# A two-block transformer kernel: the first norm's transposes moved ahead of the norm's factor, and SBUF tiles padded to 64 bytes

## The chip, the cores and the metric

The kernel runs on one NeuronCore of a Trainium2 chip. The metric is the device time of one execution in microseconds. Five engines work side by side, each through its own queue in order: TensorE (PE, with the loading of its stationary operand shown apart as PEld), VectorE (DVE), ScalarE (ACT), GpSimd (POOL) and SyncE (SP), which here only issues DMA transfers.

## What is computed

A sequence of 256 tokens of width 2048 goes through two blocks, one after the other. Only the first lines matter for the change:

```
def rmsnorm(x, w):
    xf = x.astype(jnp.float32)
    y = xf * lax.rsqrt(jnp.mean(xf * xf, axis=-1, keepdims=True) + RMS_EPS)
    return (y * w.astype(jnp.float32)).astype(x.dtype)
...
    h = x
    for l in range(DEPTH):
        u = rmsnorm(h, mix_norm_w[l])
        p = u @ w_in[l]
        o_dn = deltanet_group(p[..., :DN_COLS], ...)
        o_rw = rwkv7_group(p[..., DN_COLS:], ...)
        h = h + jnp.concatenate([o_dn, o_rw], axis=-1).astype(h.dtype) @ w_out[l]
        h = h + memory_cross_attention(...)
        h = h + squared_relu_mlp(rmsnorm(h, ffn_norm_w[l]), ffn_w1[l], ffn_w2[l])
    return rmsnorm(h, final_norm_w)
```

The second block has a gated mixer and attention of its own, and 32 experts of which a router picks two for each token.

## The kernel before

Everything is in float32. To keep its precision at TensorE's fast float32r rate, each large product is made of three: an operand is split into a high part (rounded to float32r) and the low rest, and high by high, high by low and low by high are summed in PSUM. `wsplit` (L283) does this for weights: one DMA of up to 1 MB into a tile `raw` (three buffers), then by halves an ACT cast into `wh` (L294) and a DVE subtraction into `wl` (L295). `gemm_To` (L300) takes the weights as the stationary operand and the activations `uh`, `ul` (tiles `b`) as the moving one, 256 columns at a time; `gemm_No` (L326) takes activations as the stationary and 512 columns of `wh` or `wl` as the moving operand.

The program starts in `setup` (L212): SP issues four transfers of x (rows 0 to 127 and 128 to 255, each in two halves of 1024 columns) into one `b` tile, then the constants `cst` (128x1088, the unit matrix in its first 128 columns), then the parameters `prm`. `mixers` (L870) loads a few rows, makes small parameters on DVE, and calls `norm_T` (L804), which works in a strict sequence: ACT squares x in eight pieces of 512 columns and sums each (L345); DVE adds the sums and finds the inverse root by three Newton steps on a 128x2 tile (L262 to L280); ACT and DVE multiply x by it (L811, L813); `to_T` (L366) then transposes the scaled x by 128x128 blocks on PE (L259), two blocks a chunk, and of each of the 16 chunks ACT writes the high part times the norm's weight (L372) and DVE the low part (L373).

With `uh` and `ul` the first product runs, `gemm_To` on `win_s` (272 columns of weights, L882), one matmul of 256 columns after the other through 16 chunks of depth; its 16-column group gives the gates. After it come eight units of the mixers (`rw_unit`, `dn_head`), fed by further products of `win`, then w_out, cross attention, the FFN, the second block, and at the end the experts, whose weights stream in by DMA. Beside the mixers DVE accumulates a matrix-vector product of `wmod` rows (L835), whose DMAs (L834) stand between those of `raw` in SP's queue.

The order of the instructions on each engine is fixed when the program is built: a scheduler places them by its own estimate of when their inputs are ready, and each engine then goes through its list strictly in order. A tile's address comes from its pool: tiles of a pool lie behind one another, each rounded up to 32 bytes a partition. Small tiles at the head of the pool `const` (`biases` is 16 bytes, `dnw` 4) put what follows at an odd multiple of 32 bytes: `row`, `raw`, `wh`, `wl`, and `h` in the later stages. The `b` tiles, `cst`, the FFN's `fh`, `fl` and `mraw`, the experts' `mw` and `oh` lie at a multiple of 64.

Of the kernel before, what the change touches and what calls it, by code (L numbers as in the profile page):

```python
# [88 lines left out]
CST = {}  # L89
# [96 lines left out]


class Prog:
# [23 lines left out]
    def setup(self):  # L212
        nc = self.nc
        self.bp = self.pool("b16", 3)
        self.xt = self.b16()
        for tb in range(2):
            for q in range(2):
                nc.sync.dma_start(self.xt[:, tb, q * 1024:q * 1024 + 1024], self.ins["x"][tb * 128:tb * 128 + 128, q * 1024:q * 1024 + 1024])
        self.cp = self.pool("const")
        self.rawp = self.pool("raw", 3)  # L220
        self.hlp = self.pool("hl", 3)
        ncst = CST["second"][0]
        nprm = sum(n for _, n in PRM.values())
        self.cst = self.cp.tile([128, ncst], F32, name="cst")
# [572 lines left out]
    def load_rows(self):  # L797
# [4 lines left out]
        nc.vector.tensor_scalar(self.dnw, self.p("dn_w"), 0.5, None, ALU.mult)  # L802

    def norm_T(self, src, w, uh, ul):  # L804
        nc = self.nc
        rs = self.rstd(src)
        for tb in range(2):
            for q in range(2):
                s = slice(q * 1024, q * 1024 + 1024)
                if q:  # L810
                    nc.scalar.activation(src[:, tb, s], src[:, tb, s], AF.Copy, scale=rs[:, tb:tb + 1])  # L811
                else:
                    nc.vector.tensor_scalar(src[:, tb, s], src[:, tb, s], rs[:, tb:tb + 1], None, ALU.mult)  # L813
        self.to_T([src[:, tb] for tb in range(2)], w, uh, ul)

# [43 lines left out]
    def phase1(self):  # L859
        with ExitStack() as ctx:  # L860
            self.psum(ctx, 0, {"acc": 3, "rwa": 1, "rwb": 2, "dn": 1, "dns": 1})
            self.smp = ctx.enter_context(self.tc.tile_pool(name="small1", bufs=3))
            self.rwp = ctx.enter_context(self.tc.tile_pool(name="rwp", bufs=1))
            self.dnp = ctx.enter_context(self.tc.tile_pool(name="dnp", bufs=2))
            self.scores = [self.rwp.tile([128, 2, 2, 512], F32, name=f"sc{i}") for i in range(2)]
            for a in self.scores:
                self.nc.gpsimd.memset(a, 0.0)
            return self.mixers()

    def mixers(self):  # L870
        nc = self.nc
        b16 = self.b16
        xt = self.xt
        self.load_rows()
        self.rw_params()
        self.mod_init()
        r16 = lambda a: a.rearrange("p b (k t) -> p (b k) t", t=256)
        uh, ul = r16(b16(F32R)), r16(b16(F32R))
        self.norm_T(xt, lambda c: self.p("mix_w", c), uh, ul)
        oT = r16(b16())  # L880
        acc, acg = self.mx("acc"), self.mx("dn")
# [27 lines left out]
    def b16(self, dt=F32):  # L909
        return self.bp.tile([128, 2, D], dt, tag="b16", name="b16")  # L910
# [67 lines left out]
    def xattn(self):  # L978
        nc = self.nc
        r16 = lambda a: a.rearrange("p b (k t) -> p (b k) t", t=256)  # L980
        with ExitStack() as ctx:
            P = ctx.enter_context(self.tc.tile_pool(name="xa", bufs=2))
            uh, ul = r16(self.b16(F32R)), r16(self.b16(F32R))
# [47 lines left out]
    def ffn(self, extra):  # L1031
        nc = self.nc
        r16 = lambda a: a.rearrange("p b (k t) -> p (b k) t", t=256)
        with ExitStack() as ctx:
            P = ctx.enter_context(self.tc.tile_pool(name="ffn", bufs=2))
            uh, ul = r16(self.b16(F32R)), r16(self.b16(F32R))
# [44 lines left out]
    def phase2(self, oT):  # L1081
# [9 lines left out]
        self.b2ctx = ExitStack()  # L1091
        self.b2p = self.b2ctx.enter_context(self.tc.tile_pool(name="b2rows", bufs=1))
        with ExitStack() as ctx:
            self.modp = ctx.enter_context(self.tc.tile_pool(name="modp", bufs=2))
            for q in range(4):
# [57 lines left out]
    def block2(self):  # L1153
# [3 lines left out]
        with ExitStack() as ctx:  # L1157
            P = ctx.enter_context(self.tc.tile_pool(name="b2", bufs=1))
            gmw = P.tile([128, 4, 128], F32, name="gmw")
# [597 lines left out]
    def moe(self):  # L1757
        nc = self.nc
        with ExitStack() as ctx:
            self.mxtag = "mx"  # L1760
            self.g2row = self.row_slot()
            self.row_bcast(self.modc[:, 5], self.g2row)
            K = ctx.enter_context(self.tc.tile_pool(name="kept", bufs=1))
            P = ctx.enter_context(self.tc.tile_pool(name="moe", bufs=1))
            self.load_ahead(13, P)
# [104 lines left out]
```

## Time and profile before

| | |
|---|---|
| Time, median of 3 runs | 2305.26 us (2300.73 to 2313.14) |
| The profiled execution's own time | 2314.7 us, 9.4 us over that median |
| Its span from first to last instruction | 2312.6 us |
| Busy share of the span | PE 95%, PEld 73%, DVE 64%, ACT 39%, POOL 3% |
[...]
| DMA | 575 MB, 249 GB/s over the span |

The span is cut into stages by what the engines work on: the start up to the first product (0 to 24.7 us), the first product (to 42.4 us), the mixers (to about 640 us), w_out, attention and FFN (to about 1610 us), the second block's mixer, and the experts from about 1820 us on, where the DMA engines are nearly always busy. In the timelines, an instruction's line is that of the helper that issues it; times are microseconds from the start of the span. A row of the chain of waits is one link of the work that ended last. A busy PE is not a PE at its peak, since matmuls overlap.

### The profile page before, as it was taken

To read this page: it belongs to the slowest core of one execution; us is meant where nothing else is said; L and a number is where in the kernel's file an instruction comes from. 1 tells how busy PE (TensorE), PEld (TensorE's weight loads), DVE (VectorE), ACT (ScalarE), POOL (GpSimd) and SP (SyncE) were. 2 spreads that over 40 slices of the span, in tenths; PEclk is the share of its full clock that TensorE was granted. 3 is DMA by queue.
4 is the path that set the end of the run, shared out by engine and by line. 5 is a ranking of instruction groups with operands and counts; after the bars stand their busy time and mean duration, and the time that the engine had idled before them with its cause. 6 is when DMAs were issued, how large, how long until landed. Compare 5 with 4: busy or idle time off the path is not lost.

```text
span 2312.6 us, 40957 instructions
## 1 busy us (share of the span) xinstructions
PE 2189.3 (95%) x16697; PEld 1696.1 (73%) x16697; DVE 1490.6 (64%) x2556; ACT 893.1 (39%) x1445; POOL 60.8 (3%) x166
## 2 busy tenths in 40 slices
PE   6999999999999889999999999999999989888787
PEld 6888888888787779998988989988897542233222
DVE  6778887766668788777687687756657532222223
ACT  5444443444544445434434344445555310011000
POOL 1000000010000000000000000000000000000000
PEclk9999999999899999999999999999999999999998
DMA  7425443232278776786686786754445798999997
GB/s 252 147 95 181 158 163 134 95 113 93 74 264 312 266 275 250 277 310 259 247 316 251 280 290 253 277 184 170 164 148 199 293 401 367 408 390 425 426 425 319
DMA packets 101622, 575.23 MB, mean 249 GB/s; under 512 B 11548, under 2 KB 12700, under 8 KB 45880
## 3 DMA queue, kind: packets, MB, share of 16 engines
q1 hardware_dynamic: 101432, 572.60, 65.6%
q8 instruction: 132, 2.16, 0.4%
q14 instruction: 58, 0.48, 0.1%
HBM read 570.45 MB, written 2.10 MB: 248 GB/s over the span
## 4 chain that ended last, share of the span: by engine, by line
PE 78%; DMA 11%; DVE 7%; ACT 2%; issue 2%; SPq 0%; DVEq 0%; ACTq 0%
PE acc L255 45%; PE mx L255 31%; DMA mw<-wgu 4%; PE mx L259 2%; DMA mw<-wd 2%; DMA b<-wgu 2%; DVE wl L295 1%; DMA mraw<-wmod 1%; DMA raw<-wd 1%; DVE macc L835 1%; DMA row<-wmod 0%; DMA raw<-win_s 0%; DMA raw<-wout 0%; DVE b L373 0%; ACT wh L294 0%
## 5 line engine op out<-in xcount | busy, mean ns | idle before, releaser
L294 ACT CAST wh<-raw 128x1024 fp32r<-128x1024 f32 (+1 forms) x496 | 516.3, 1043 | 722.2 <-PE acc L255 536.5
L295 DVE TENSOR_TENSOR wl<-raw,wh 128x1024 fp32r<-128x1024 f32 (+1 forms) x496 | 600.4, 1214 | 205.7 <-ACT wh L294 201.9
L255 PE MATMUL acc<-b,wh 128*128 128x256 f32 x2560 | 467.7, 283 | 1.0 <-ACT b L372 1.0
L255 PE MATMUL mx<-b,wh 128*128 128x256 f32 (+1 forms) x2016 | 414.1, 295 | 0.7 <-ACT wh L294 0.7
L255 PEld LDWEIGHTS acc<-b,wh 128*128 128x128 f32 x2560 | 398.1, 189 | 3.2 <-ACT b L372 1.7
L255 PE MATMUL acc<-b,wl 128*128 128x256 f32 x1280 | 363.8, 284 | 0.8 <-DVE wl L295 0.7
L255 PEld LDWEIGHTS mx<-b,wh 128*128 128x128 f32 (+1 forms) x2016 | 320.2, 190 | 11.5 <-issue 3.3
L255 PE MATMUL mx<-b,wl 128*128 128x256 f32 (+1 forms) x1008 | 297.4, 295 | 0.8 <-DVE wl L295 0.8
L255 PEld LDWEIGHTS acc<-b,wl 128*128 128x128 f32 x1280 | 241.3, 189 | 1.6 <-DVE wl L295 1.4
L835 DVE SCALAR_TENSOR_TENSOR macc<-mraw,silc,macc 128x1024 f32<-128x1024 f32 x160 | 205.0, 1282 | 54.2 <-DMA mraw<-wmod 53.4
L255 PE MATMUL acc<-wh,fh 128*128 128x512 f32 x512 | 204.3, 399 | 0.0
L255 PE MATMUL acc<-wh,fl 128*128 128x512 f32 x512 | 202.2, 395 | 0.0
L255 PE MATMUL acc<-wl,fh 128*128 128x512 f32 x512 | 201.0, 393 | 0.0
L255 PEld LDWEIGHTS mx<-b,wl 128*128 128x128 f32 (+1 forms) x1008 | 191.4, 190 | 5.0 <-DVE wl L295 1.1
L255 PE MATMUL mx<-mw,xs 128*32 128x512 f32 (+1 forms) x512 | 126.3, 656 | 21.2 <-DMA mw<-wgu 21.1
L255 PE MATMUL acc<-wh,b 128*128 128x512 f32 x384 | 124.3, 402 | 1.0 <-ACT row L976 1.0
L255 PEld LDWEIGHTS acc<-wh,fl 128*128 128x128 f32 x512 | 96.1, 188 | 24.4
L255 PEld LDWEIGHTS acc<-wl,fh 128*128 128x128 f32 x512 | 96.2, 188 | 23.2 <-DVE wl L295 0.2
L255 PEld LDWEIGHTS acc<-wh,fh 128*128 128x128 f32 x512 | 96.1, 188 | 22.0
L255 PE MATMUL mx<-raw,xs 128*32 128x512 f32 (+1 forms) x328 | 95.9, 625 | 10.0 <-DMA raw<-wgu 10.0
L1590 DVE SCALAR_TENSOR_TENSOR eth<-eth,mx 128x256 f32<-128x256 f32 x9 | 3.8, 421 | 145.3 <-ACT eth L1589 145.3
L255 PEld LDWEIGHTS mx<-mw,xs 128*32 128x32 f32 (+1 forms) x512 | 26.9, 120 | 84.6 <-issue 43.8
(490 smaller groups left out, 2823.1 us busy)
## 6 DMA issues: line engine op xcount, KB each, us to landing
raw<-w SPq DMA_DIRECT2D x128, 1024.0 KB, 5.6
mraw<-wmod SPq DMA_DIRECT2D x160, 512.0 KB, 5.0
raw<-win SPq DMA_DIRECT2D x76, 1024.0 KB, 4.9
mw<-wgu SPq DMA_DIRECT2D x62, 1024.0 KB, 14.3
raw<-wgu SPq DMA_DIRECT2D x40, 1024.0 KB, 14.5
mw<-wd SPq DMA_DIRECT2D x28, 1024.0 KB, 14.5
raw<-wout SPq DMA_DIRECT2D x24, 1024.0 KB, 5.9
b<-wgu SPq DMA_DIRECT2D x23, 1024.0 KB, 10.8
```

What stands on the lines that cost most here:

```text
L255: return self.nc.tensor.matmul(out, lhsT=lhsT, rhs=rhs, start=start, stop=stop, skip_group_check=True)
L259: return self.nc.tensor.transpose(out, in_, self.ident[:k, :k])
L294: nc.scalar.copy(h[:, :n], rs)
L295: nc.vector.tensor_tensor(l[:, :n], rs, h[:, :n], ALU.subtract)
L835: nc.vector.scalar_tensor_tensor(a, b, self.silc[:, k:k + 1], a, ALU.mult, ALU.add)
L1590: nc.vector.scalar_tensor_tensor(th[:n], th[:n], 1.0, ps[:n, 0:256], ALU.add, ALU.mult)
```

## The change

Three things change at the start. `setup` loads the unit matrix (the first 128 columns of `cst`) ahead of x, x by halves of its columns (first half of both row blocks, then the second), then `prm`, and the rest of `cst` behind it. `norm_T` comes ahead of `load_rows`, `rw_params` and `mod_init` in the program, and is written anew: three matmuls of zeros come first; the squares are divided between ACT (first row block) and DVE (second); the transposes take x as it is, before its factor is known, into seven PSUM banks and, once the first is free, an eighth; the factor is laid along the row by two matmuls (a row sum of the unit matrix scaled by it, so that each partition has all 256 factors) and copied to a 128x256 tile `row` by ACT; and each chunk then takes three instructions where it took two: DVE multiplies transposed x by weight and `row` into `f` (L863), ACT casts `f` into `uh` (L864), DVE subtracts into `ul` (L865).

Besides, every pool hands out SBUF tiles through a class `Lines`, which widens a tile whose size is an odd multiple of 32 bytes to the next multiple of 64, and gives a view of it. All SBUF tiles then start at a multiple of 64 bytes.

```diff
+class Lines:
+    def tile(self, shape, dt, **kw):
+        n = int(np.prod(shape[1:]))
+        size = mybir.dt.size(dt)
+        full = -(-n * size // 64) * 64 // size
+        if -(-n * size // 32) % 2 == 0:
+            return self.pool.tile(shape, dt, **kw)
+        t = self.pool.tile([shape[0], full], dt, **kw)[:, 0:n]
...
-        return self.ctx.enter_context(self.tc.tile_pool(name=name, bufs=bufs, **kw))
+        return Lines(self.ctx.enter_context(self.tc.tile_pool(name=name, bufs=bufs, **kw)))
...
-        for tb in range(2):
-            for q in range(2):
+        self.cst = self.cp.tile([128, ncst], F32, name="cst")
+        nc.sync.dma_start(self.cst[:, 0:128], self.ins["cst"][:, 0:128])
+        for q in range(2):
+            for tb in range(2):
                 nc.sync.dma_start(self.xt[:, tb, q * 1024:q * 1024 + 1024], self.ins["x"][tb * 128:tb * 128 + 128, q * 1024:q * 1024 + 1024])
...
-        nc.sync.dma_start(self.cst, self.ins["cst"][:, :ncst])
         nc.sync.dma_start(self.prm, self.ins["prm"])
+        nc.sync.dma_start(self.cst[:, 128:ncst], self.ins["cst"][:, 128:ncst])
...
     def norm_T(self, src, w, uh, ul):
         nc = self.nc
-        rs = self.rstd(src)
+        t1 = lambda: self.rwp.tile([128, 256], F32, tag="t1", name="t1", bufs=12)
+
+        z = self.hlp.tile([128, 1024], F32, tag="wl", name="zero")[:, 0:512]
+        nc.vector.memset(z, 0.0)
+        ps = self.mx("dns")
+        for _ in range(3):
+            self.mm(ps, z[:, 0:128], z)
+        ss = self.smp.tile([128, 2, 4], F32, tag="ss", name="ss")
+        for q in range(4):
+            for tb in range(2):
+                junk = self.hlp.tile([128, 1024], F32, tag="wh", name="junk")[:, 0:512]
+                s = src[:, tb, q * 512:q * 512 + 512]
+                if tb:
+                    nc.vector.scalar_tensor_tensor(junk, s, 1.0, s, ALU.mult, ALU.mult, accum_out=ss[:, tb, q:q + 1])
+                else:
+                    nc.scalar.activation(junk, s, AF.Square, accum_out=ss[:, tb, q:q + 1])
+        rs = self.rstd_from(ss)
...
+        ts = [transposed(j, tag) for j, tag in enumerate(("acc", "acc", "acc", "rwa", "rwb", "rwb", "dn"))]
+        ps = self.mx("dns")
         for tb in range(2):
-            for q in range(2):
-                s = slice(q * 1024, q * 1024 + 1024)
-                if q:
-                    nc.scalar.activation(src[:, tb, s], src[:, tb, s], AF.Copy, scale=rs[:, tb:tb + 1])
-                else:
-                    nc.vector.tensor_scalar(src[:, tb, s], src[:, tb, s], rs[:, tb:tb + 1], None, ALU.mult)
-        self.to_T([src[:, tb] for tb in range(2)], w, uh, ul)
+            self.mm(ps[:, tb * 128:tb * 128 + 128], rs[:, tb:tb + 1].to_broadcast([128, 128]), self.ident, start=(tb == 0))
+        row = t1()
+        nc.scalar.copy(row, ps[:, 0:256])
+        for j in range(8):
+            for c in range(2):
+                k = j * 2 + c
+                f = t1()
+                nc.vector.scalar_tensor_tensor(f, ts[j][:, c * 256:c * 256 + 256], w(k), row, ALU.mult, ALU.mult)
+                nc.scalar.copy(uh[:, k, :], f)
+                nc.vector.tensor_tensor(ul[:, k, :], f, uh[:, k, :], ALU.subtract)
+            if j == 0:
+                ts.append(transposed(7, "acc"))
```

The built programs show where this puts the instructions. On DVE, the list before goes from the root's last step to the scaling of x, the 16 low parts of the norm, and then the low parts of the first weights:

```order
L278 SCALAR_TENSOR_TENSOR rs_y<-rs_b,rs_y 128x2
L813 TENSOR_SCALAR b_58<-b_58,rs_y 128x1024 x2
L373 SCALAR_TENSOR_TENSOR b_111<-mx,prm,b_110 128x256 x16
L295 TENSOR_TENSOR wl<-raw,wh 128x544 x3
L835 SCALAR_TENSOR_TENSOR row<-row,silc 128x512 x2
L295 TENSOR_TENSOR wl<-raw,wh 128x544
```

In the changed list 32 instructions stand in their place, 16 of L863 and 16 of L865 in alternating groups of three or four, and this is the end of them (`t` is `f`, `b_98` is `ul`, `b_97` is `uh`):

```order
L863 SCALAR_TENSOR_TENSOR t_253<-mx,prm,t_186 128x256
L865 TENSOR_TENSOR b_98<-t_245,b_97 128x256
L865 TENSOR_TENSOR b_98<-t_249,b_97 128x256
L865 TENSOR_TENSOR b_98<-t_253,b_97 128x256
L315 TENSOR_TENSOR wl<-raw,wh 128x544 x3
L888 SCALAR_TENSOR_TENSOR row<-row,silc 128x512 x2
L315 TENSOR_TENSOR wl<-raw,wh 128x544
```

The low parts of the weights (L295 before, L315 now) still come behind all of the norm's work on this engine. On PE, the first product's list before starts right behind the 32 transposes, with four matmuls on the first weights' high part and then one on `wl`:

```order
L259 MATMUL mx<-cst,b_58 128x128 x32
L255 MATMUL mx<-b_110,wh 128x256
L255 MATMUL mx<-b_111,wh 128x256
L255 MATMUL mx<-b_110,wh 16x256
L255 MATMUL mx<-b_111,wh 16x256
L255 MATMUL mx<-b_110,wl 128x256
```

Now the zeros, 28 transposes, the factor's two matmuls and the last four transposes stand ahead of it, and the product itself begins with the same five:

```order
L275 MATMUL mx<-zero 128x512 x3
L279 MATMUL mx<-cst,b_58 128x128 x28
L275 MATMUL mx<-cst,rs_y 128x128 x2
L279 MATMUL mx<-cst,b_58 128x128 x4
L275 MATMUL mx<-b_97,wh 128x256
L275 MATMUL mx<-b_98,wh 128x256
L275 MATMUL mx<-b_97,wh 16x256
L275 MATMUL mx<-b_98,wh 16x256
L275 MATMUL mx<-b_97,wl 128x256
```

What moved is the transposes, from behind the factor to ahead of it; the fifth matmul of the product still needs the first `wl`. On SP, a part of its list before, from the fourth transfer of `win_s` on:

```order
L834 DMA row<-wmod 128x512 x2
L287 DMA raw<-win 128x2048
L834 DMA row<-wmod 128x512
L287 DMA raw<-win 128x2048
L834 DMA row<-wmod 128x512
L287 DMA raw<-win 128x2048
L834 DMA row<-wmod 128x512 x3
L287 DMA raw<-win 128x2048
```

and the same part now:

```order
L887 DMA row<-wmod 128x512 x2
L307 DMA raw<-win 128x2048
L887 DMA row<-wmod 128x512
L307 DMA raw<-win 128x2048
L887 DMA row<-wmod 128x512 x2
L307 DMA raw<-win 128x2048
L887 DMA row<-wmod 128x512 x2
L307 DMA raw<-win 128x2048
```

The transfers are the same; the rows of `wmod` stand elsewhere between those of `win`. In the mixers, too, the scheduler places a number of instructions differently against one another; from w_out on the lists agree but for line numbers.

## Rows read from the trace of the kernel before

**Rows 1.** The page of the whole span: engines' busy time, then the chain's shares.
```profile
PE 2189.3 (95%) x16697; PEld 1696.1 (73%) x16697; DVE 1490.6 (64%) x2556; ACT 893.1 (39%) x1445; POOL 60.8 (3%) x166
...
PE 78%; DMA 11%; DVE 7%; ACT 2%; issue 2%; SPq 0%; DVEq 0%; ACTq 0%
```
**Rows 2.** The chain that ended last, first 60 us: start, length, what.
```profile
4.78 9.37 DMA raw<-win_s
...
14.95 6.00 PE mx L259 x26
...
21.49 2.49 DVE b L373 x6
...
23.98 0.64 DVE wl L295
...
24.66 17.73 PE mx L255 x137
...
46.88 3.60 DMA row<-wmod
```
**Rows 3.** Timeline, 0 to 45 us: start, length, engine, line, out<-in, count.
```profile
2.71 0.56 SPq L226 DMA_DIRECT2D cst<-cst  x1
...
8.61 0.60 ACT L345 ACTIVATE mx<-b 128x512 f32<-128x512 f32 x1 [1.27 <-DMA b<-x]
...
9.89 0.60 ACT L345 ACTIVATE mx<-b 128x512 f32<-128x512 f32 x1
...
11.26 0.16 DVE L360 TENSOR_REDUCE s<-ss 128x2 f32<-128x8 f32 x1 [10.31 <-ACT mx L345]
...
16.24 2.65 ACT L372 ACTIVATE b<-mx,prm 128x256 fp32r<-128x256 f32 x7
...
23.89 1.99 DVE L295 TENSOR_TENSOR wl<-raw,wh 128x544 fp32r<-128x544 f32 x3
...
25.80 1.53 DVE L835 SCALAR_TENSOR_TENSOR row<-row,silc 128x512 f32<-128x512 f32 x2
```
**Rows 4.** The same chain of waits, at 43 us: two subtractions of 256 columns.
```profile
43.04 0.76 DVE t L461 x2
```
**Rows 5.** Groups by shape, whole span: count, busy us, mean ns, idle before.
```profile
L255 PE MATMUL mx<-b,wh 128*128 128x256 f32 x1984 | 409.0, 295 | 0.7 <-ACT wh L294 0.7
...
L255 PE MATMUL mx<-oh,b 128*128 128x256 f32 x256 | 36.2, 290 | 4.6 <-DVE xs L1521 3.1 <-DVE h L1630 1.5
...
L378 DVE TENSOR_TENSOR y<-ey,y 128x512 fp32r<-128x512 f32 x36 | 24.7, 687 | 2.9 <-ACT y L377 1.4
...
L1055 DVE TENSOR_TENSOR fl<-fy,fh 128x512 fp32r<-128x512 f32 x32 | 20.6, 686 | 0.0
...
L1119 ACT CAST b<-tab 128x256 fp32r<-128x256 f32 x16 | 6.0, 403 | 2.4 <-DVE tab L1118 2.3
```
**Rows 6.** The page's DMA issues: count, KB each, us to landing.
```profile
mw<-wgu SPq DMA_DIRECT2D x62, 1024.0 KB, 14.3
...
raw<-wgu SPq DMA_DIRECT2D x40, 1024.0 KB, 14.5
```
**Rows 7.** Busy us (count) of each engine by stretch; PEclk is the granted clock.
```profile
22.00:24.00 2.00, 1.17 (x6) 0.62 (x6) 2.00 (x6) 2.00 (x6) 0.00 (x0) 1.00 0.00 0
...
24.00:26.00 2.00, 1.33 (x6) 1.27 (x7) 2.00 (x4) 0.54 (x1) 0.00 (x0) 0.58 0.00 0
...
28.00:30.00 2.00, 2.00 (x19) 1.87 (x18) 1.39 (x2) 0.56 (x2) 0.00 (x0) 1.00 0.77 249
...
1200.00:1240.00 40.00, 40.00 (x335) 39.96 (x334) 24.77 (x24) 16.86 (x19) 0.16 (x1) 1.00 0.70 256
...
1520.00:1560.00 40.00, 40.00 (x173) 32.15 (x172) 21.84 (x22) 14.79 (x15) 0.00 (x0) 1.00 0.54 185
```
**Rows 8.** Groups by shape again: two of the products with 512 moving columns.
```profile
L255 PE MATMUL acc<-wh,fh 128*128 128x512 f32 x512 | 204.3, 399 | 0.0
...
L255 PE MATMUL acc<-wh,b 128*128 128x512 f32 x384 | 124.3, 402 | 1.0 <-ACT row L976 1.0
```

More of the change, by code (lines that the diff above doesn't have):

```diff
@@ L184, in pack, with __init__ @@
     return o
+class Lines:
+    def __init__(self, pool):
+        self.pool = pool
+    def tile(self, shape, dt, **kw):
[5 more added lines that the diff above has]
+        t = self.pool.tile([shape[0], full], dt, **kw)[:, 0:n]
+        if len(shape) == 2:
+            return t
+        names = "abcd"[:len(shape) - 1]
+        return t.rearrange(f"p ({' '.join(names)}) -> p {' '.join(names)}", **dict(zip(names, shape[1:])))
 class Prog:
@@ L215, in setup @@
         self.xt = self.b16()
-        for tb in range(2):
-            for q in range(2):
+        self.cp = self.pool("const")
+        ncst = CST["second"][0]
+        self.cst = self.cp.tile([128, ncst], F32, name="cst")
+        nc.sync.dma_start(self.cst[:, 0:128], self.ins["cst"][:, 0:128])
+        for q in range(2):
+            for tb in range(2):
                 nc.sync.dma_start(self.xt[:, tb, q * 1024:q * 1024 + 1024], self.ins["x"][tb * 128:tb * 128 + 128, q * 1024:q * 1024 + 1024])
-        self.cp = self.pool("const")
         self.rawp = self.pool("raw", 3)
         self.hlp = self.pool("hl", 3)
-        ncst = CST["second"][0]
         nprm = sum(n for _, n in PRM.values())
-        self.cst = self.cp.tile([128, ncst], F32, name="cst")
         self.prm = self.cp.tile([128, nprm], F32, name="prm")
-        nc.sync.dma_start(self.cst, self.ins["cst"][:, :ncst])
         nc.sync.dma_start(self.prm, self.ins["prm"])
+        nc.sync.dma_start(self.cst[:, 128:ncst], self.ins["cst"][:, 128:ncst])
         self.biases()
@@ new lines, in norm_T, with transposed @@
+        rs = self.rstd_from(ss)
+        def transposed(j, tag):
+            t = self.mx(tag)
+            for c in range(2):
+                k = j * 2 + c
+                for tb in range(2):
+                    self.tr(t[:, c * 256 + tb * 128:c * 256 + tb * 128 + 128], src[:, tb, k * 128:k * 128 + 128])
+            return t
+        ts = [transposed(j, tag) for j, tag in enumerate(("acc", "acc", "acc", "rwa", "rwb", "rwb", "dn"))]
+        ps = self.mx("dns")
+        for tb in range(2):
+            self.mm(ps[:, tb * 128:tb * 128 + 128], rs[:, tb:tb + 1].to_broadcast([128, 128]), self.ident, start=(tb == 0))
@@ new lines, in norm_T @@
+        row = t1()
+        nc.scalar.copy(row, ps[:, 0:256])
+        for j in range(8):
+            for c in range(2):
+                k = j * 2 + c
+                f = t1()
[4 more added lines that the diff above has]
+                ts.append(transposed(7, "acc"))
@@ L861, in phase1 @@
             self.psum(ctx, 0, {"acc": 3, "rwa": 1, "rwb": 2, "dn": 1, "dns": 1})
-            self.smp = ctx.enter_context(self.tc.tile_pool(name="small1", bufs=3))
-            self.rwp = ctx.enter_context(self.tc.tile_pool(name="rwp", bufs=1))
-            self.dnp = ctx.enter_context(self.tc.tile_pool(name="dnp", bufs=2))
+            self.smp = Lines(ctx.enter_context(self.tc.tile_pool(name="small1", bufs=3)))
+            self.rwp = Lines(ctx.enter_context(self.tc.tile_pool(name="rwp", bufs=1)))
+            self.dnp = Lines(ctx.enter_context(self.tc.tile_pool(name="dnp", bufs=2)))
             self.scores = [self.rwp.tile([128, 2, 2, 512], F32, name=f"sc{i}") for i in range(2)]
@@ L873, in mixers @@
         xt = self.xt
+        r16 = lambda a: a.rearrange("p b (k t) -> p (b k) t", t=256)
+        uh, ul = r16(b16(F32R)), r16(b16(F32R))
+        self.norm_T(xt, lambda c: self.p("mix_w", c), uh, ul)
         self.load_rows()
@@ L981, in xattn @@
         with ExitStack() as ctx:
-            P = ctx.enter_context(self.tc.tile_pool(name="xa", bufs=2))
+            P = Lines(ctx.enter_context(self.tc.tile_pool(name="xa", bufs=2)))
             uh, ul = r16(self.b16(F32R)), r16(self.b16(F32R))
@@ L1091, in phase2 @@
         self.b2ctx = ExitStack()
-        self.b2p = self.b2ctx.enter_context(self.tc.tile_pool(name="b2rows", bufs=1))
+        self.b2p = Lines(self.b2ctx.enter_context(self.tc.tile_pool(name="b2rows", bufs=1)))
         with ExitStack() as ctx:
-            self.modp = ctx.enter_context(self.tc.tile_pool(name="modp", bufs=2))
+            self.modp = Lines(ctx.enter_context(self.tc.tile_pool(name="modp", bufs=2)))
             for q in range(4):
@@ L1157, in block2 @@
         with ExitStack() as ctx:
-            P = ctx.enter_context(self.tc.tile_pool(name="b2", bufs=1))
+            P = Lines(ctx.enter_context(self.tc.tile_pool(name="b2", bufs=1)))
             gmw = P.tile([128, 4, 128], F32, name="gmw")
@@ L1762, in moe @@
             self.row_bcast(self.modc[:, 5], self.g2row)
-            K = ctx.enter_context(self.tc.tile_pool(name="kept", bufs=1))
-            P = ctx.enter_context(self.tc.tile_pool(name="moe", bufs=1))
+            K = Lines(ctx.enter_context(self.tc.tile_pool(name="kept", bufs=1)))
+            P = Lines(ctx.enter_context(self.tc.tile_pool(name="moe", bufs=1)))
             self.load_ahead(13, P)
```

5 lines of the change are left out of this document (1 added, 4 removed).

## The prediction

> **What bounds the kernel now.** I read the page first. PE is busy for 2189.3 of 2312.6 us, and the chain that ended last lies on PE for 78% and on DMA for 11% [rows 1]. So time won or lost before PE's first product reaches the end almost whole: the mixers are a chain on PE, and the experts' stage cannot start before them. Next I read that chain over the first 60 us [rows 2]: x lands, ACT squares it (the row that names win_s covers the squares and the root), DVE scales, PE transposes from 14.95 us, DVE writes low parts until 23.98, then the first `wl`, and from 24.66 PE multiplies for 17.73 us without a break, until 42.40. This is the stretch that the change rewrites. What ends last in it is not PE but DVE: the product cannot get past its fifth matmul until DVE has made the first `wl`, and in DVE's list that stands behind all of the norm's work.
>
> **The start, step by step.** All times are of the profiled execution.
>
> 1. x. The transfer of the unit matrix goes ahead of x on SP; a transfer of `cst` took SP 0.56 us to issue [rows 3]. ACT waited for the third piece of x until 8.61 and took the fourth at 9.89 without a wait [rows 3], so the fourth had landed by 9.89 and now lands by about 10.4. `prm` moves ahead of the rest of `cst` and is there earlier than now; the rest of `cst` is wanted only after the first product, over 30 us later, so its delay costs nothing.
>
> 2. Squares. ACT's row block is first and ends earlier. DVE squares the fourth piece in two instructions of 512 columns; the nearest row is two products of that form in 1.53 us [rows 3]. So the sums are complete at about 11.9, against 11.26 now: dividing the squares gains nothing, since the last piece of x sets the end.
>
> 3. The root. From the reduction at 11.26 [rows 3] to 14.15, where the row of 9.37 us ends that began at 4.78 [rows 2], are 2.9 us, with small parameter instructions between, as in the changed list. Factor at 14.8.
>
> 4. The factor along the row. Two small matmuls and an ACT copy of 256 columns, whose nearest row is a cast of 403 ns [rows 5]. For the matmuls and their passage to ACT no row stands alone; from 0.4 us (two places in the row of 26 transposes in 6.00 us [rows 2]) to 1.3 us (first transpose at 14.95 [rows 2] to ACT's first reading at 16.24 [rows 3], which holds several of them). I take 0.8, the middle, as there are two of them and their result has to pass to ACT. The row is ready at 14.8 + 0.8 + 0.4 = 16.0, between 15.6 and 16.5.
>
> 5. The norm on DVE. Scaling (L811, L813) goes, but each chunk has two DVE instructions instead of one. Out of PSUM, six of 256 columns took 2.49 us [rows 2], 0.415 each; two SBUF subtractions of 256 columns took 0.76 us [rows 4], 0.38 each. 16 x (0.415 + 0.38) = 12.7 us, so DVE is through at 28.7; now it is at 23.98. The 16 ACT casts of 403 ns [rows 5], 6.4 us in all, run beside it. Three `wl` of the first weights took 1.99 us [rows 3], so the first is done at 29.4, where it was at 24.62 [rows 2]. **The product starts 4.8 us later, although the transposes are long done.** The transposes and the zeros are hidden before it on PE; the scalings on ACT that go away were not waited for, and DVE's two are counted by letting its work on the chunks start at 16.0, right behind the row.
>
> 6. The clock. The granted clock stood at 0.58 in the stretch from 24 to 26 us and at full before and from 28 on; in the stretch before it fell, PE had been busy for 1.17 of 2 us [rows 7]. [...]
>
> The sum is 4.8 + 0.5 = **5.3 us later**. The ends: with the row at 15.6, every DVE instruction at 0.38 and nothing for the clock, 4 us; with 16.5, each at 0.42 and 2 us for the clock, 8 us. The later `wl` follow without a break and PE needs 2 us for each, so the rest of the product keeps its pace. SP's first transfers behind it wait for buffers that `wl` frees, and move with it.
>
> **The alignment.** It reaches everything, so I looked for pairs of rows of one instruction at an odd and an even multiple of 32 bytes. DVE's subtraction of 512 columns takes 686 ns into `fl` (even) and 687 into `y` (odd). The transfers into `mw` (even) and `raw` (odd) land in 14.3 and 14.5 us [rows 6]. A matmul of 256 columns takes 290 ns when both operands are even (`oh`) and 295 when the weights are odd (`wh`) [rows 5]; the latter is a mean over stretches with waits. Only the 512-column products, whose moving operand is `wh` or `wl`, have no even counterpart. 40 us hold 335 matmuls of 256 columns and 173 of 512 [rows 7]: 119.4 and 231.2 ns. One with an odd moving operand takes less than two with an even one. So I take **nothing** for the alignment. [...]
>
> **The mixers.** The scheduler's lists differ there in some places, with the same instructions. Nothing in them is shorter; a few waits move. I take nothing, plus or minus 5 us.
>
> The profiled execution would go from 2314.7 to 2320.0 us. It lies 9.4 us over the median of the runs, 2305.26; from that median the same 5.3 us give **2310.6 us**. Under 0.5% (11.5 us) is about what a measurement of this kernel cannot tell from no change, and the forecast is on that side.
>
> **Rivals.**
>
> [...]
>
> *The start gains after all.* If DVE's two instructions a chunk cost as little as the one does now, 6.7 us, `wl` would be ready at 23.3 and the product start 1.3 us earlier: 2304 us. Two instructions would have to overlap wholly; the six in a row above [rows 2] do not. This is also the case where the change does what its words say.
>
> *The mixers' queues lose (slower).* DVE's accumulations of `wmod` stand in its list ahead of work that PE wants, and each waits for a transfer that SP issues between those of `win`. One such wait stood 3.60 us in the chain at 46.88 [rows 2]. SP's list is now ordered otherwise there. With one more such wait in each of four units, 4 x 3.6 = 14.4 us, the time is 2305.26 + 5.3 + 14.4 = 2325 us, slower by 0.9%. It decides if SP reaches a row of `wmod` later than DVE does, two times or more: 5.3 + 2 x 3.6 is already 12.5. Against it: DVE is busy for 64% only [rows 1], and the new list splits the group of three rows of `wmod` that stood ahead of a transfer of `win`.
>
> **How the numbers follow.** Forecast 0.52, alignment 0.22, start gains 0.10, mixers lose 0.16. The forecast and the start's gain lie within 0.5%: 0.62 the same. The alignment gives 13.3 us less, faster, 0.22; the mixers slower, 0.16. The range reaches to the rivals on both sides, with 5 us of the mixers' uncertainty below the one at 2292 us: 2287 us; above, to the third rival, 2325 us. The forecast's own range is 4 to 8 us plus and minus 5: 2304 to 2318 us.
>
> **What the changed profile would show.** Right: transposes from about 6 us, the norm's DVE instructions from about 16 to 28.7 us, the first `wl` at about 29 us, the first product from 29 to about 47.5 us and its first microseconds at 1.2 GHz; 512-column matmuls still 173 in 40 us of the FFN; DVE's 512-column subtraction still 686 ns. Wrong: a product that starts before 25 us, or more than 176 matmuls of 512 columns in 40 us, or new DMA rows of `wmod` in the chain between 50 and 640 us.

## The result: half a per cent slower, and the profile after

The changed kernel takes 2315.94 us in the median of 20 runs (2310.36 to 2324.63); the kernel before, run beside it, 2303.02 us (20 runs, 2297.75 to 2313.14). The medians lie 12.9 us apart; the ratio of the runs is 1.0051, 95% interval 1.0038 to 1.0063: 11.7 us slower, between 8.8 and 14.5, just at the bound of 0.5%. The forecast was 5.3 us. The two profiled executions hide this: that of the changed kernel took 2313.92 us, 2.0 under its median, that of before 2314.7, 11.7 over the median of its 20 runs. Their spans, 2312.2 and 2312.6 us at mean granted clocks of 0.980 and 0.979, agree by chance, so the traces are compared stage by stage here.

The page of the changed kernel, its busy times and the chain's shares; they answer to [rows 1] and tell little: PE is busy for 0.3% of the span less, and the chain lies on DVE for 2% more:

```profile
PE 2182.5 (94%) x16707; PEld 1694.3 (73%) x16707; DVE 1496.9 (65%) x2579; ACT 889.1 (38%) x1436; POOL 59.4 (3%) x166
...
PE 77%; DMA 9%; DVE 9%; ACT 2%; issue 2%; SPq 0%; DVEq 0%; ACTq 0%
```

The chain that ended last at the start of the changed kernel (start, length, what), against [rows 2]:

```profile
13.98 0.17 DVE rs_y L298
14.15 0.14 issue
14.29 1.21 PE mx L275 x4
15.52 0.38 ACT t L858
15.92 1.66 DVE t L863 x4
17.58 1.34 DVE b L865 x4
...
27.56 0.72 DVE wl L315
...
28.33 18.51 PE mx L275 x137
...
55.37 2.33 issue
```

("issue" is time in which the engine waits for nothing that the profile shows.) The transposes, which start at 6.56 us now, are gone from the chain. In their place stands DVE, from 15.92 to 27.28 us, with the norm's 32 instructions; then comes the first `wl`, and only then PE. The product ends at 46.84 us, where it ended at 42.39: **4.45 us later**. But the trace of before is itself late at this point. Five other runs below have its start, and in four of them PE was granted the full clock where it had 0.58 from 24 to 26 us ([rows 7]); address_only, in the chain and in that stretch:

```profile
24.50 16.16 PE mx L255 x137
```

```profile
24.00:26.00 2.00, 1.50 (x12) 1.45 (x13) 2.00 (x4) 0.37 (x1) 0.00 (x0) 1.00 0.00 0
```

In these four the product's result is copied at 40.2 to 40.7 us, in the fifth (split_pair) at 41.9, in before at 42.4; in the four kernels with the changed start (this one, front_only, after_64, front_and_64) at 46.4 to 47.2. The means, 41.0 and 46.9, are **5.8 us apart**. Busy time and granted clock (PEclk, last but two) by stretch show PE's state at that point, against [rows 7]:

```profile
20.00:22.00 2.00, 0.00 (x0) 0.00 (x0) 2.00 (x7) 1.01 (x4) 0.00 (x0) 0.50 0.00 0
28.00:30.00 2.00, 1.67 (x8) 1.60 (x9) 2.00 (x4) 0.00 (x0) 0.00 (x0) 0.50 0.08 15
32.00:34.00 2.00, 2.00 (x13) 1.79 (x13) 1.39 (x2) 0.20 (x1) 0.00 (x0) 0.60 0.76 256
34.00:36.00 2.00, 2.00 (x20) 1.88 (x19) 0.67 (x2) 0.65 (x1) 0.00 (x0) 1.00 0.72 270
```

PE stands idle at 20 us with the granted clock at 0.50, and the product starts at that level: 13 matmuls in 2 us at 0.60, 20 at full clock.

In the FFN nothing moved. Windows of 40 us, the first inside a group of 256-column products, the second inside one of 512 columns (PE's count is in the first brackets), against the last two of [rows 7]:

```profile
1288.00:1328.00 40.00, 40.00 (x336) 40.00 (x335) 27.31 (x26) 16.75 (x18) 0.00 (x0) 1.00 0.74 275
1334.00:1374.00 40.00, 40.00 (x174) 32.43 (x173) 35.77 (x36) 15.99 (x16) 0.00 (x0) 1.00 0.80 288
```

That is the pace of before (335 and 173). So the start accounts for 4.5 us of 11.7 by this pair of traces and for 5.8 by all of them, and the padding, whose effect had been put at nothing, did not pay. The experiments ask what the other 6 to 7 us are, and whether addresses matter at all.

### The profile page after: what moved, and what is told of

Its sections match the earlier page's. It is cut to its first block, busy times and chain, and to the rows that moved or that the text cites. A ratio compares the mean times of both kernels' runs of the same rounds, so it can differ in the third digit from the quotient of the medians.

```text
span 2312.2 us, 40991 instructions
## 1 busy us (share of the span) xinstructions
PE 2182.5 (94%) x16707; PEld 1694.3 (73%) x16707; DVE 1496.9 (65%) x2579; ACT 889.1 (38%) x1436; POOL 59.4 (3%) x166
## 4 chain that ended last, share of the span: by engine, by line
PE 77%; DMA 9%; DVE 9%; ACT 2%; issue 2%; SPq 0%; DVEq 0%; ACTq 0%
PE acc L275 43%; PE mx L275 32%; DMA mw<-wgu 4%; DMA mw<-wd 2%; PE mx L279 2%; DVE wl L315 1%; DMA mraw<-wmod 1%; DVE macc L888 1%; DMA raw<-wd 1%; DMA b<-wgu 1%; ACT wh L314 0%; DVE ey L1673 0%; DMA raw<-wq 0%; DMA b<-x 0%; DVE itt L424 0%
## 5 line engine op out<-in xcount | busy, mean ns | idle before, releaser
L315 DVE TENSOR_TENSOR wl<-raw,wh 128x1024 fp32r<-128x1024 f32 (+1 forms) x496 | 600.1, 1213 | 206.4 <-ACT wh L314 203.3
L275 PEld LDWEIGHTS acc<-b,wl 128*128 128x128 f32 x1280 | 246.1, 192 | 1.9 <-DVE wl L315 1.7
L275 PE MATMUL mx<-mw,xs 128*32 128x512 f32 (+1 forms) x512 | 120.9, 633 | 23.2 <-DMA mw<-wgu 23.2
```

The source lines that it names most:

```text
L275: return self.nc.tensor.matmul(out, lhsT=lhsT, rhs=rhs, start=start, stop=stop, skip_group_check=True)
L315: nc.vector.tensor_tensor(l[:, :n], rs, h[:, :n], ALU.subtract)
```

## The experiments

The FFN is a good place to measure PE's pace, since PE never waits there for long: 0.7 us in all in the kernel before. Its length below is taken from the first squared relu (L1051 in the kernel before) to the last addition to `h` (L948): 711.0 us before, 711.3 in the changed kernel. "Distance" is the place of `wh` and `wl` minus that of the other operand of the same product, modulo 256 bytes (where modulo 128 is meant it is said). A window's count takes in the matmuls that lie across its ends, some two of them, so 40 us divided by it comes out 0.5 to 1.5% short; a pace in ns below is the mean from start to start in groups of 384 matmuls of 256 columns or 192 of 512 (six of each stand apart in the FFN). The large products are in float32r; in the kernel before a matmul of 256 columns has a mean row of 295 ns in float32r (`b`, `wh`, [rows 5]) and of 394 in plain float32 (`t`, `cst`). Where a row gives a wide range, the groups of one trace differ.

| kernel | distance from `b` | from `fh`, `fl` | 256-column matmuls in 40 us | 512-column | FFN, us | median, us | ratio to before, 95% |
|---|---|---|---|---|---|---|---|
| before | 160 | 96 | 335 | 173 | 711.0 | 2303 to 2307 | 1 |
| changed | 0 | 128 | 336 | 171 to 174 | 711.3 | 2315.94 | 1.0051 (1.0038 to 1.0063) |
| front_only | 160 | 96 | - | - | 710.7 | 2310.26 | 1.0029 (1.0011 to 1.0047) |
| padding_only | 0 | 128 | 336 | 173 | 710.0 | 2309.16 | 1.0007 (0.9994 to 1.0020) |
| address_only | 192 | 64 | 342 to 345 | 176, 177 | 697.6 | 2292.60 | 0.9947 (0.9927 to 0.9967) |
| weights_with_norm | 160 | 96 | - | - | 710.7 | 2300.26 | 0.9976 (0.9961 to 0.9992) |
| after_64 | 64 | 64 | 342 to 356 | 174, 177 | 695.3 | 2294.09 | 0.9949 (0.9929 to 0.9969) |
| pair_128 | 0 | 64 | 335, 336 | 176, 177 | 704.7 | 2297.80 | 0.9961 (0.9939 to 0.9983) |
| split_pair (`wh` and `wl`) | 192 and 0 | 0 and 64 | 342, 343 | 174 | 705.0 | 2295.20 | 0.9957 (0.9934 to 0.9979) |
| norm_and_64 | 192 | 64 | - | - | 698.1 | 2287.32 | 0.9923 (0.9891 to 0.9954) |
| address_192 | 64 | 64 | 342 to 356 | 176, 177 | 689.6 | 2282.18 | 0.9897 (0.9871 to 0.9922) |
| norm_and_192 | 64 | 64 | 334 to 347 | 176, 177 | 696.8 | 2281.20 | 0.9889 (0.9868 to 0.9909) |
| front_and_64 | 192 | 64 | - | - | 699.1 | 2297.10 | 0.9959 (0.9940 to 0.9979) |

### front_only: the change without the padding

```diff
-        if -(-n * size // 32) % 2 == 0:
+        if True:
             return self.pool.tile(shape, dt, **kw)
```

> The change without the padding: every tile has the address and the size that the pools give it, and behind the first product every engine has the same list as before. Theory A (two costs: the front starts the first product about 4.5 us later, and the padding, which changes the scheduler's lists in the mixers, costs the other 8 us): 4 to 6 us over before, about 2308 us, first product's end 4.4 us later, and the mixers no longer than before. Theory B (the front alone costs all of it, by the clock or by what it does to the transfers behind it): 11 to 15 us over before, about 2316 us. Theory C (the odd and even addresses cost the rest): as A here, 4 to 6 us.

1.0029 times before: 6.7 us slower, between 2.5 and 10.8 (the medians lie 4.1 us apart). The first product's result is copied at 47.23 us instead of 42.42. The list of DVE there is that of the changed kernel, and so, within 0.3 us, is its timing: the norm from 16.23 us on, the first `wl` at 27.86. This is what A and C expect; B's 11 to 15 us lie above the interval. The front costs about what was forecast, 5.3 us.

### padding_only: the kernel before with the class Lines

```diff
+class Lines:
...
-        return self.ctx.enter_context(self.tc.tile_pool(name=name, bufs=bufs, **kw))
+        return Lines(self.ctx.enter_context(self.tc.tile_pool(name=name, bufs=bufs, **kw)))
```

> The kernel before with the padding alone: all SBUF tiles on multiples of 64 bytes, the start as before, and the mixers' lists as in the changed kernel. Theory A: 6 to 9 us over before, about 2311 us, all of it in the mixers, 42 to 640 us, and nothing in the FFN. Theory B: no change, 0 plus or minus 2 us. Theory C: 6 to 9 us, spread over w_out, the FFN and the second block as well. The rival of the prediction by which alignment pays: 10 to 20 us under before.

1.0007, no difference that can be measured (1.6 us slower, between -1.4 and 4.6; the medians lie 3.0 us apart); A's 6 to 9 us are not there, and the FFN is as long as before. Yet the traces show longer mixers in two pairs. Windows from the first product's end to the last unit's end, in this kernel and then in pair_128 (below), whose `wh` and `wl` have the same addresses but whose lists are those of before:

```profile
40.31:666.22 625.91, 606.12 (x7554) 527.04 (x7553) 478.00 (x1233) 299.55 (x636) 44.32 (x139) 0.99 0.38 136
```

```profile
40.17:659.32 619.15, 603.18 (x7554) 524.32 (x7553) 476.23 (x1233) 297.99 (x636) 45.36 (x139) 1.00 0.39 137
```

The same 7554 matmuls take 6.8 us more: 3.8 of it is idle time of PE (19.8 against 16.0), and 2.9 is PE being busy for longer, at a slightly lower mean clock. The changed kernel and front_only, which differ by the padding alone, stand to each other in the same way, 629.77 and 621.11 us:

```profile
46.86:676.63 629.77, 610.35 (x7554) 531.56 (x7553) 477.16 (x1231) 299.44 (x636) 43.20 (x139) 0.98 0.38 135
```

```profile
47.23:668.34 621.11, 605.04 (x7554) 525.47 (x7553) 475.19 (x1231) 298.15 (x636) 43.42 (x139) 0.99 0.38 136
```

PE's waits in the same two stretches (what was waited for, us in total, times, longest), the changed kernel and then front_only:

```profile
PE mx L275 <- issue: 5.2, 4, 2.3
PE mx L275 <- DVE it L426: 1.9, 4, 0.7
...
PE mx L275 <- DVE rs_y L298: 1.0, 2, 0.8
```

```profile
PE mx L275 <- issue: 3.3, 4, 1.3
...
PE mx L275 <- DVE it L426: 0.7, 2, 0.4
```

The padding widens small tiles of the mixers too and hands out views of them, and the scheduler puts steps of the inversion (`it`) and of a root (`rs_y`) elsewhere on DVE; which of the padded tiles does it was not tried. In the two pairs of traces the mixers are 6.8 and 8.7 us longer, of which 3.8 and 3.3 are idle time of PE. The rest goes with the granted clock, which stood at 0.50 for 10.2 and 20.5 us of the padded mixers (means of 0.99 and 0.98 in the rows above), and for 3.4 and 6.8 of the others (1.00 and 0.99). That cannot be laid to the padded lists, since the mixers of the kernel before had 27.3 us of it. Over all traces the difference is less: the three with the padded lists (padding_only, the changed kernel, after_64) took 625.9, 629.8 and 627.0 us for the mixers; of the seven with the lists of before, five took 616.0 to 624.1, and two, the kernel before itself and split_pair, 628.8 and 629.8. The means are 627.6 and 622.6, **5 us apart**, and four of the seven also have `wh` and `wl` at the distances that prove faster below. In the two long ones of the seven the mean granted clock of the mixers is 0.98, in address_only, front_only and pair_128 0.99 to 1.00. In the kernel before it stood at 0.50 for some 20 us from 608 us on:

```profile
608.00:612.00 4.00, 4.00 (x61) 3.39 (x59) 1.32 (x5) 2.94 (x3) 1.73 (x6) 0.50 0.00 0
612.00:616.00 4.00, 4.00 (x40) 3.23 (x39) 1.10 (x1) 1.81 (x4) 0.00 (x0) 0.50 0.02 4
628.00:632.00 4.00, 3.87 (x29) 2.87 (x30) 3.35 (x8) 3.39 (x11) 0.00 (x0) 0.94 0.00 0
```

How often that happens in runs without a profile is not known, nor whether it is why padding_only stands so near to before. So the traces suggest some 4 us for the padded lists, and no run shows them.

### address_only: the addresses alone

```diff
         self.dnw = self.cp.tile([128, 1], F32, name="dnw")
+        self.cp.tile([128, 8], F32, name="pad")
...
+        self.hlp.tile([128, 8], F32, tag="pad", name="pad", bufs=1)
         self.mem_kv()
```

Two tiles of 32 bytes that nothing reads or writes. Every engine's list stays that of before.

> The kernel before with two dead tiles of 32 bytes, one behind dnw and one behind wl, so that row, raw, wh and wl stand at multiples of 64 bytes; every engine's list is that of before, instruction for instruction. Theory A: no change, 0 plus or minus 2 us, and 335 matmuls of 256 columns and 173 of 512 in 40 us of the FFN as before. Theory B: the same. Theory C: 6 to 9 us over before. The rival by which alignment pays: 10 to 20 us under before, and over 176 matmuls of 512 columns in 40 us.

**0.9947: 12.2 us faster**, between 7.6 and 16.8. No theory of mine had this: A and B said nothing, C said slower; only the case in which the alignment pays, to which the prediction gave 0.22, had it, at 10 to 20 us. The same two kinds of window as above:

```profile
1174.00:1214.00 40.00, 40.00 (x342) 40.00 (x341) 26.44 (x24) 16.72 (x18) 0.00 (x0) 1.00 0.76 277
...
1309.00:1349.00 40.00, 40.00 (x177) 32.81 (x176) 35.65 (x36) 16.17 (x17) 0.12 (x1) 1.00 0.81 291
```

From start to start a matmul of 256 columns takes 117.8 ns instead of 120.0, one of 512 columns 229.4 instead of 233.8; the FFN takes 697.6 us, 13.4 less than 711.0. But in padding_only `wh` and `wl` lie at multiples of 64 as well, and gain nothing. The multiple of 64 is not what counts. What differs is that here they lie 64 bytes off a multiple of 128, and `b`, `fh` and `fl` on one; in padding_only all lie on one. This gave theories P and Q of the next runs.

### weights_with_norm: the first product taken chunk by chunk with the norm

```diff
+        ws = itertools.chain(*(self.wsplit(src, ncol) for src in srcs))
+        with self.tc.issue_after(self.squared), self.tc.issue_after(self.rooted):
+            ready = [next(ws) for _ in range(4)]
+        for k in steps:
...
+                _, h, l = ready[0]
+                for i, (a, b) in enumerate(((h, uh), (h, ul), (l, uh))):
+                    self.mm(outs[m], a[:, sl], b[:, k, :], start=(k == 0 and i == 0 and m % 2 == 0),
...
+            ready += list(itertools.islice(ws, 1))
```

`steps` yields after each chunk of the norm. It stands on front_only. Two PSUM banks are kept free for the product, so the transposes go ahead into five banks instead of seven, and DVE's accumulations of `wmod` come behind the norm.

> The front of the change without the padding, and the first product taken chunk by chunk with the norm: the first weights' low parts stand between the norm's instructions on DVE instead of behind all of them, two PSUM banks are kept free for the product, and the accumulations of wmod come behind the norm. If DVE's list was what held the product (theories A and C), DVE has 16 x 0.73 + 8 x 0.66 = 17 us of work from 16 us on, PE follows it and the first product ends at about 36 us, where it ended at 42.4 before and 46.9 in the changed kernel; the time is 5 to 7 us under before, about 2298 us, plus or minus 7 us for the mixers, whose lists shift again. If PE's clock held it (theory B), the product ends no earlier than 44 us and the time is not under before.

0.9976: 5.5 us faster, between 1.8 and 9.0. The timeline of DVE shows the low parts of the weights between the norm's instructions (start, length, line, out<-in), and ACT's copy of the finished product:

```profile
15.89 0.88 DVE L883 SCALAR_TENSOR_TENSOR t<-mx,prm,t 128x256 f32<-128x256 f32 x2 [1.78 <-ACT t L877]
16.69 1.35 DVE L315 TENSOR_TENSOR wl<-raw,wh 128x544 fp32r<-128x544 f32 x2
...
20.44 0.76 DVE L885 TENSOR_TENSOR b<-t,b 128x256 fp32r<-128x256 f32 x2
22.93 0.73 DVE L315 TENSOR_TENSOR wl<-raw,wh 128x544 fp32r<-128x544 f32 x1 [1.74 <-ACT wh L314]
...
38.41 0.59 ACT L494 COPY praw<-mx 128x512 f32<-128x512 f32 x1 [1.36 <-PE mx L275]
```

The product is copied at 38.41 us, 8.8 earlier than in front_only (47.23), 4.0 earlier than in the trace of before and 1.8 to 2.3 earlier than in the four with its start at full clock. The 36 us expected were missed by 2.4: DVE now waits 1.74 us for a `wh` of ACT, which is busy for 0.57 of the 2 us from 20 us on, while PE is busy throughout at a granted clock of 0.50; that PE gave the buffer of `wh` back late is the author's estimate from these rows. DVE's list, and not PE's clock in the main, held the product: A and C, not B.

### after_64, pair_128 and split_pair: which distance counts

All three are pairs of dead tiles as in address_only, with other sizes: 64 and 64 bytes in the changed kernel; 96 and 32 in the kernel before; 32 and 32 there, with a third of 64 between `wh` and `wl`.

> The changed kernel with two dead tiles of 64 bytes, one behind dnw and one behind wl: row, raw, wh and wl move from a multiple of 128 to an odd multiple of 64, all else keeps its place modulo 128, and every engine's list stays that of the changed kernel. Theory P (a product runs faster when its moving and its stationary operand lie 64 bytes apart modulo 128): the FFN, 711 us before and in the changed kernel and 698 in the run with the addresses alone, goes to about 698, and the time from 2316 to about 2303 us, no longer over before. Theory Q (what pays is wh and wl at an odd multiple of 64, wherever the other operand lies): the same. Theory R (the gain of that run came from something else): 2316 us, FFN 711.

0.9949, 11.8 us faster than before, where the changed kernel is 11.7 slower: **128 bytes of dead tiles turn it by some 23 us.** Theory R falls. The FFN's 695.3 us are 16 less, a little more than the 13 expected.

> The kernel before with dead tiles of 96 bytes behind dnw and 32 behind wl: wh and wl at multiples of 128, as b is, while fh and fl stay at an odd multiple of 64; lists as before. Theory P: the FFN's 256-column matmuls (wh or wl with b, no distance) stay at 120 ns, and its 512-column ones (wh or wl with fh or fl, 64 apart) go from 234 to about 229; the FFN about 704 us and the time about 2299. Theory Q: both as slow as before, FFN 711, 2306 us. Theory R: 2306 us.

The FFN took 704.7 us and the time is 2297.80, both as P has it. The windows show it twice over, in one kernel:

```profile
1270.00:1310.00 40.00, 40.00 (x336) 40.00 (x335) 26.06 (x24) 16.71 (x18) 0.00 (x0) 1.00 0.76 273
1316.00:1356.00 40.00, 40.00 (x177) 32.82 (x176) 34.97 (x35) 16.25 (x17) 0.00 (x0) 1.00 0.80 277
```

The 256-column products, whose operands are both on a multiple of 128, keep the slow pace (336); the 512-column ones, whose `fh` and `fl` lie 64 off, have the fast one (177). `wh` and `wl` are the same tiles in both, so it is the distance of two operands and not the place of one: Q falls.

> As the run with the addresses alone, with 64 bytes more between wh and wl: wh at an odd multiple of 64, wl at a multiple of 128, b at a multiple of 128, fh and fl at an odd multiple of 64; lists as before. Theory P: of the 256-column matmuls those that wait for a load of wh run at 117.5 ns and those for wl at 120; of the 512-column ones those that move wl run fast (under 230) and those that move wh slowly (232 or more); FFN about 704 us. Theory Q: what has wh is fast and what has wl is slow in both kinds, so the 512-column ones come out the other way round. Theory R: all as before.

The length, 705.0 us, is what P gives, but by luck: the split that P expected between matmuls on `wh` and on `wl` is in neither kind. The 512-column products come out alike, 174 in 40 us, 232.5 ns each whichever of the two they move:

```profile
1282.00:1322.00 40.00, 40.00 (x343) 40.00 (x341) 27.89 (x27) 16.77 (x18) 0.00 (x0) 1.00 0.77 281
1327.00:1367.00 40.00, 40.00 (x174) 32.38 (x173) 34.71 (x36) 16.24 (x17) 0.23 (x1) 1.00 0.78 281
```

and there are as many 256-column ones as in address_only, so those that load `wl` are fast too, at no distance from `b`. So the distance orders whole kernels in which `wh` and `wl` lie alike, and is not yet a rule for the single matmul. Whether it is the loading of the next stationary operand beside the running stream that suffers, or something else, stays open.

### norm_and_64, address_192, norm_and_192, front_and_64

norm_and_64 and front_and_64 add the two tiles of address_only to weights_with_norm and to front_only; address_192 and norm_and_192 have 160 and 32 bytes, on the kernel before and on weights_with_norm.

> The first product taken chunk by chunk with the norm, as in the run of that name, with the two dead tiles of 32 bytes of the run with the addresses alone. Theories P and Q: the two gains add, 5.9 us from the start and 13.5 from the products, about 2287 us, 0.8% under before. Theory R: 2300 us as without the tiles.

2287.32 us: the gains add as expected. In after_64, with `wh` and `wl` on the other side of `b`, two of the FFN's six groups of 384 matmuls of 256 columns had taken 43.4 us, where address_only's took 45.1; hence the next two.

> The kernel before with dead tiles of 160 bytes behind dnw and 32 behind wl: wh and wl 64 bytes behind b modulo 256, as in the changed kernel with two tiles of 64, where the run with the addresses alone has them 64 bytes ahead; lists as before. Theory P (only the distance modulo 128 counts): 256-column matmuls at 117.5 ns and 512-column ones at 229, FFN 698, 2293 us. Theory P2 (the side counts too): 256-column ones at 115 ns, FFN 690 to 696, 2285 to 2291 us.

**0.9897: 23.8 us faster than before**, between 18.0 and 29.8, and a little more than P2 gave. The windows, one of 256 columns, one of 512, and another of 256:

```profile
1255.00:1295.00 40.00, 40.00 (x356) 40.00 (x355) 27.79 (x27) 17.84 (x19) 0.00 (x0) 1.00 0.81 290
1298.00:1338.00 40.00, 40.00 (x176) 32.83 (x175) 36.22 (x37) 16.27 (x17) 0.27 (x1) 1.00 0.82 295
```

```profile
1343.00:1383.00 40.00, 40.00 (x342) 40.00 (x342) 26.88 (x25) 16.72 (x18) 0.00 (x0) 1.00 0.77 276
```

355 or 356 matmuls of 256 columns stand in four of the six groups, 113.4 ns each, against 117.8 in address_only and 120.0 before; but 342 stand in the group at 1343 us, at the same addresses, and 346 in the sixth. The 512-column ones stay where they were. So at a distance of 64 PE can take a second, faster pace, and does not always take it. Of 18 such groups in the three kernels at 64, six ran at it throughout (four here, two in after_64); of 18 in the three at 192, none. The side of `b` seems to matter, then, but what lets PE into the faster pace stays open.

> The first product taken chunk by chunk with the norm, with the dead tiles of 160 and 32 bytes. Theory P: 2287 us, as with the tiles of 32 bytes. Theory P2: 2280 to 2285 us.

2281.20 us, the fastest measured, but only 1 us from address_192, which the intervals do not separate. The first product's result is copied at 38.06 us against 40.66 in address_192, and the FFN takes 7 us more (696.8 against 689.6): none of its six groups of 384 runs at 113.4 ns throughout. In the kernels with the new start, whose zeros take a buffer of `wl` first, `wl` lies ahead of `wh` in SBUF; in address_192 it lies behind, at the same distances modulo 256. Whether that decides between the two paces was not tried.

> The change without the padding, as in the run of the front alone, with the two dead tiles of 32 bytes of the run with the addresses alone: it has that run's addresses, and behind the first product its lists. If the front costs its 4.4 to 6.7 us whatever the addresses are, 2297 to 2300 us; if the front's cost came from the odd addresses, 2293 us.

2297.10 us, 4.5 over address_only in the medians and 2.7 by the two ratios; the interval (2293 to 2302 us) takes in both expectations, and the run does not decide. The traces do: the first product's result is copied at 46.36 us against 40.68 in address_only, 5.7 later, so the front costs as much at good addresses.

## Why the prediction held, and where its terms were off

The sign, the mechanism at the start and the range held (2287 to 2325 us); the predicted 2310.6 us are 5.3 under the result. Part of that nearness is luck: the forecast stood on a median of three runs, 2.2 us above that of the 20 beside the result. Of the 11.7 us between the two kernels it had 5.3; the rest came from a start somewhat dearer than forecast and, as far as the traces show, from the mixers, which it put at nothing; only the 5 us allowed there brought the result into its own range of 2304 to 2318 us. Whether the time would lie within 0.5% was a toss-up, with 0.51% measured.

- *x and the squares.* DVE's two squares begin at 10.14 us and the reduction at 11.56, predicted 11.9; before it stood at 11.26. Right: dividing the squares gains nothing.
- *The root and the row.* The factor is there at 14.15 (predicted 14.8, the step's 2.9 us being 2.6), but the matmuls and the copy took 1.6 us instead of 1.2, with the granted clock at 0.50 from 14 us on. DVE starts at 15.92, predicted 16.0.
- *The norm on DVE.* 32 instructions in 11.36 us, where 12.7 were predicted: in a row they take 0.355 us each, less than rows of one kind gave ([rows 2, 4]). The first `wl` is done at 28.28, predicted 29.4: 3.7 us later than before instead of 4.8.
- *The clock.* The product took 18.51 us instead of 17.73: 0.8, predicted 0.5. No run shows the 0.5 us that the forecast adds for it; what the runs showed in its place is 0.8 us in this pair and more against other traces. The product of before itself lost some 1.5 us, at a granted clock of 0.50 from 24.66 to 27.70 us; in four of the five others with that start it ran at full clock and took 16.1 to 16.3 us, so against these the clock costs the new start some 2 us, the upper bound that the prediction gave. In the changed kernel PE is idle from 20 to 26 us, the clock stands at 0.50 from 14 to 32 us, and the matmuls of zeros did not keep it up until the product. The forecast of the profile puts the clock in GHz; the traces give it as a share of full speed alone. The front's sum, 4.45 us in the pair of traces, 5.8 over all of them and 6.7 in the runs, was forecast as 5.3.
- *The mixers.* "I take nothing, plus or minus 5 us" is the step that was off. The mixers with the padded lists are 5 us longer over all traces, 6.8 and 8.7 in the two pairs, about half of it by waits of PE and the rest by a clock that also falls without the padding (0.50 for 27.3 us in the mixers of before). With the front's 5.8 that is 11 to 15 us, around the 11.7 measured; by the runs of the two parts alone, 6.7 and 1.6, it would be 8.3, and the 3.4 between lie within their intervals. So the front is shown by runs, and the padding's share is argued from traces. The form that the rival of the mixers' queues gave this cost was wrong: no transfer of `wmod` stands in the changed kernel's chain between 40 and 680 us, where before had two, one of them the 3.60 us of [rows 2].
- *The alignment.* "Nothing" was right for this padding: 336 and 171 to 174 matmuls, 711.3 us. Its reasoning was not: it compared odd and even places of one operand, row by row, and no such pair can show what counts here, the distance between two operands. The other case, to which the prediction gave 0.22, that an alignment pays, was right that 13 us and more lay in the pace of these products: in address_only the FFN is 13.4 us shorter, at 117.8 ns for 256 columns and 229.4 for 512 instead of 120.0 and 233.8. No run shows the 13.3 us that it was put at; the runs showed nothing for this padding and 12.2 us for address_only. This padding is not how to get them: it moved `wh` and `wl` from one slow distance from `b` (160) to another (0). 12.2 and 23.8 us at unchanged lists show that something about the addresses matters; no run shows by what mechanism.

## What to carry to other kernels

An engine that is made to wait for less starts earlier only if what it waits for last gets earlier: here the transposes came 8 us earlier and the product later, since the low parts of its weights stood behind more work on DVE. Interleaving two producers on the engine that both need (2 to 4 us earlier than before) did what moving one of them did not. A single trace can be off by more than the change is worth: that of before had a fall of the clock to 0.50 for 3 us in the very stretch that was rewritten, and another for 20 us in the mixers. And before a change of addresses is judged, try the distances between the two operands of the products with dead tiles that leave every list as it is; it is a change of a line or two, and here worth up to 1%.

## What the runs showed that was not expected

Matmuls of the same shape, behind one another and at full clock, ran in these kernels at a pace that changed with where their two operands lie to each other in SBUF: for 256 columns 120.0 ns at distances of 0 and 160 bytes modulo 256, 117.8 at 192, and at 64 either 117.8 or 113.4, group by group; for 512 columns 233.8 ns at 96 and 128, 229.4 at 64. In split_pair, where `wh` and `wl` lie at different distances, each kind has one pace of its own, 117.8 and 232.5, which the distances alone do not give. At unchanged lists the pace changed with the place of one operand (pair_128 and padding_only have `wh` and `wl` at the same addresses, and 229.4 and 233.7 ns for 512 columns with `fh` and `fl` moved by 64 bytes), but no run shows that the loading of the next weights is what collides. The row of a single matmul hardly shows it: 282 ns before and 277 in address_192 for the 256-column products of the FFN, and for the 512-column ones 399 ns before ([rows 8]) and 395:

```profile
L255 PE MATMUL acc<-b,wh 128*128 128x256 f32 x1825 | 314.0, 277 | 0.0
...
L255 PE MATMUL acc<-wh,fh 128*128 128x512 f32 x507 | 200.2, 395 | 0.0
```

Overlapping matmuls are to be counted over a stretch, from start to start, and not read by their mean length.
